# The GLU's first block: four output tiles in shared PSUM banks, multiplied inside the steps of the state-space layer

## The chip, the cores and the metric

The kernel runs on one core of one Trainium2 chip. The metric is the device time of one launch in microseconds (us). Three runs of the kernel before took 2366.6, 2366.81 and 2368.81 us; the median is 2366.81 us. One more execution was profiled and took 2366.55 us; its span between the first and the last instruction is 2364.6 us, and every row below is from it.

## What is computed

The reference is a decoder trunk of two layers on 16 meta tokens and 256 real tokens of width 2048. Layer 0 mixes by attention and a short convolution, layer 1 by a state-space layer (S5) and a gated linear unit (GLU); after each comes a SwiGLU feed-forward network (FFN). The change lies in layer 1, in the state-space layer and the GLU:

```python
# s5_mixer(u, ...), u: (1, 272, 2048)
_, _, x_re, x_im = lax.associative_scan(_complex_affine_combine, (a_r, a_i, bu_re, bu_im), axis=1)
y = einsum('blgp,ghp->blgh', x_re, c_re) - einsum('blgp,ghp->blgh', x_im, c_im)
y = y.reshape(Bsz, L, D_MODEL) + d_skip * uf
g = jax.nn.gelu(y)
return (g @ w_glu1) * jax.nn.sigmoid(g @ w_glu2)      # both weights 2048 x 2048
```

## The kernel before

**Products.** Activations lie transposed in SBUF, as 16 tiles of 128 channels by the tokens. Each is split into a high and a low part (`xh`, `xl`, type fp32r), each weight chunk too (`whi`, `wlo`), and one product of the reference is three matmuls: hi with `xh`, hi with `xl`, lo with `xh` (`mm3`, L297 to L299). The weights come in the order of a plan (class `Weights`): SyncE (SP) loads a chunk into one of four raw buffers, ScalarE (ACT) rounds it to `whi` (L102), VectorE (DVE) subtracts to get `wlo` (L109), both into four buffers. `next` hands a chunk out and first lets `pump` bring casts, subtractions and loads up to `W.ahead` (SA = 3) chunks on. A GLU chunk holds two of the 16 input tiles for all output tiles of its block: three output tiles make it 128x768.

**State-space steps.** The layer works on 16 tiles k of eight groups each. `s5_step(i)` issues for each stage of its list the tile k = i - lag (L1332 on): loads of a tile's tables (`w`, `w2`, `kt`), `f_u` (DVE scales the input), `f_c` (32 small matmuls, L1200), `f_mod` (DVE and GpSimd (POOL) rotate them, L843), `f_scan` (two scans on DVE, L1226, and a rotation), `f_y` (48 small matmuls, L1241 and L1246, into one two-bank tile), `f_yt` (DVE transposes that tile, L1252, which frees it), and the GELU in `f_g1` to `f_g3` over POOL, ACT and DVE. `f_g2` writes `xh` of tile k at step k + 7, `f_g3` writes `xl` at step k + 8. The last stage of tile 15 is in step 23.

**Where steps and GLU meet.** The loop at L1340 issues steps -1 to 17; nothing of the GLU is in them, except that a pump at step 15 brings one cast and one subtraction. Steps 18 to 23 are put into the tick queue `queues[1]` and run, with pauses, between the chunks of the GLU's first block. `GLU_BLOCKS` has four blocks of three output tiles and two of two, each with one PSUM bank per output tile and gate. The order of the chunks in a block is `GLU_ORDER`. When a block's first sums (for the sigmoid) are done, ACT takes their tanh, and DVE multiplies the second sums by it (`gate`); each result is squared for the norm. After the first block everything is drained and PSUM is given out anew.

**Engines.** Each engine works through its own list in order, and the order of issue in the program is that list's order; SP's loads also wait in order, each for its buffer.

Of the kernel before, what the change touches and what calls it, by code (L numbers as in the profile page):

```python
# [10 lines left out]
F32 = mybir.dt.float32  # L11
# [3 lines left out]
AF = mybir.ActivationFunctionType  # L15
ALU = mybir.AluOpType
AX = mybir.AxisListType
PSUM = bass.MemoryType.PSUM
DRAM = bass.MemoryType.DRAM

P = 128
D = 2048
KT = D // P
NMETA = 16
NREAL = 256
# [12 lines left out]
NE = EB + (NC + EB - 1) // EB  # L38
NCP = EB * (NE - EB)
QC = 4 * NC  # L40
GLU_BLOCKS = [(0, 3), (3, 6), (6, 9), (9, 12), (12, 14), (14, 16)]

LOG2E = 1.4426950408889634
LN2_HI = 0.693359375
# [14 lines left out]
WB = 4  # L59
RB = 4  # L60
SA = 3
# [79 lines left out]
def trunk(  # L141
# [5 lines left out]
    nc = tc.nc  # L147
# [8 lines left out]
    W = Weights(nc, raws, parts)  # L156

    def rows(w):
        return w.rearrange("(k p) c -> p k c", p=P)
# [44 lines left out]
    plan_ffn(0)  # L204

    GLU_ORDER = [(c, i) for c in range(6) for i in range(2)] + [(6, 0), (7, 0), (6, 1), (7, 1)]
    for a, b in GLU_BLOCKS:
        for c, i in GLU_ORDER:
            W.add(rows((s5_w_glu2, s5_w_glu1)[i][0])[:, 2 * c:2 * c + 2, a * P:b * P], (2, (b - a) * P))
    plan_ffn(1)  # L210

# [13 lines left out]
    xh = keep.tile([P, KT, NT], F32R, name="xh")  # L225
    xl = keep.tile([P, KT, NT], F32R, name="xl")
# [33 lines left out]
    psm = ps_scope.enter_context(tc.tile_pool(name="psm", bufs=3, space=PSUM))  # L260
# [6 lines left out]
    def bank():  # L267
        return psm.tile([P, 512], F32, tag="mm", name="mm")
# [27 lines left out]
    def mm3(ps, hi, lo, bh, bl, first, last):  # L296
        nc.tensor.matmul(ps, hi, bh, start=first, stop=False)  # L297
        nc.tensor.matmul(ps, hi, bl, start=False, stop=False)  # L298
        nc.tensor.matmul(ps, lo, bh, start=False, stop=last)  # L299
# [77 lines left out]
    queues = [deque() for _ in range(3)]  # L377

    def tick():
        for q in queues:  # L380
            if q:
                for f in q.popleft():
                    f()

    def drain():
        while any(queues):
            tick()

    def warm(func):

        nc.scalar.activation(warm_t, eps_t, func)
# [293 lines left out]
    osq = Squares(KT)  # L685
# [5 lines left out]
    ps2_scope = ExitStack()  # L691
    psm = ps2_scope.enter_context(tc.tile_pool(name="psm2", bufs=8, space=PSUM))
# [116 lines left out]
    CW0 = EW0 + 8 * NCP  # L809
    SCR = CW0 + 8 * 16 * (T + 1)  # L810
# [28 lines left out]
    def ts(o, a, s1, s2, o0, o1, eng=None):  # L839
        (eng or V).tensor_scalar(o, a, s1, s2, op0=o0, op1=o1)  # L840

    def tt(o, a, b, op, eng=None):
        (eng or V).tensor_tensor(o, a, b, op=op)  # L843
# [4 lines left out]
    M_, A_, S_ = ALU.mult, ALU.add, ALU.subtract  # L848
# [304 lines left out]
    osq = ffn(m, Sandwich(m, 0, 1, osq, (0, 2), NT), NT)  # L1153
# [8 lines left out]
    sp_scope = ExitStack()  # L1162
    sp = sp_scope.enter_context(tc.tile_pool(name="sp", bufs=2))
    sps_scope = ExitStack()
    sps = sps_scope.enter_context(tc.tile_pool(name="sps", bufs=1, space=PSUM))
    spx_scope = ExitStack()
    spx = spx_scope.enter_context(tc.tile_pool(name="spx", bufs=3, space=PSUM))

    d0 = [sp.tile([P, 4, NC], F32, name=f"d0{a}", bufs=1) for a in range(2)]
    for a in range(2):  # L1170
# [130 lines left out]
    def read_u(g):  # L1301
        nc.sync.dma_start(out=m_flat[:, 4 * NT * g:4 * NT * (g + 1)], in_=ub[g])

    for k in range(KT + 2):
# [14 lines left out]
        if k == KT + 1:  # L1319
# [3 lines left out]
            for t in range(4):  # L1323
                p = slice(32 * t, 32 * t + 32)
                v = xt[p, :NT].rearrange("p (c s) -> p c s", s=T)
# [6 lines left out]
              (f_g1, 6), (f_scan, 3), (f_yt, 5), (f_y, 4)]  # L1332
    ahead = {f_load: 3, f_load2: 2}

    def s5_step(i):
        for f, lag in stages:
            k = i - lag
            if ahead.get(f, 0) <= k < KT:
                f(k)

    for i in range(-1, KT + 2):
        if i == KT - 1:
            W.pump()
        s5_step(i)
        if i in (2, 4):
            read_u(i // 2 + 1)
    spx_scope.close()


    for i, pause in zip(range(KT + 2, KT + 8), (0, 2, 2, 1, 1, 1)):  # L1350
        queues[1].extend([[]] * pause + [[lambda i=i: s5_step(i)]])
    psg_scope = ExitStack()
    psm = psg_scope.enter_context(tc.tile_pool(name="psg", bufs=6, space=PSUM))
    ps2_scope = ExitStack()
    mr = m[:, :, :NREAL]

    osq = Squares(KT, cols=NREAL)
    ths = {}
    for a, b in GLU_BLOCKS:
        n = b - a  # L1360
        p2 = [bank()[:, :NREAL] for _ in range(n)]
        p1 = [bank()[:, :NREAL] for _ in range(n)]
        now = a == 0 or b == KT
        if b == KT:
            drain()

        def gate(o, a=a, p1=p1):
            tt(mr[:, a + o], p1[o], ths[a][:, o], M_)
            osq.add(mr[:, a + o])
        for c, i in GLU_ORDER:  # L1370
            hi, lo = W.next()
            if c == 7 and i == 1:
                ts(th[:, :n], th[:, :n], 0.5, 0.5, M_, A_)
                if b == KT:
                    warm(AF.Sqrt)
            for o in range(n):
                for k in range(2):
                    kt = 2 * c + k
                    mm3((p2, p1)[i][o], hi[:, k, o * P:(o + 1) * P], lo[:, k, o * P:(o + 1) * P],
                        xh[:, kt, :NREAL], xl[:, kt, :NREAL], kt == 0, kt == KT - 1)  # L1380
                if c == 7 and i == 1 and now:
                    gate(o)
            if c == 7 and i == 0:
                if a == 0:
                    th = sp.tile([P, SCR - CW0], F32, tag="w2", name="th", bufs=3)[:, :3 * NREAL].rearrange("p (o n) -> p o n", o=3)
                else:
                    th = sg.tile([P, 3, NREAL], F32, tag="th", name="th")
                ths[a] = th
                for o in range(n):
                    nc.scalar.activation(th[:, o], p2[o], AF.Tanh, scale=0.5)  # L1390
            tick()
        if not now:
            queues[0].extend([[lambda o=o, g=gate: g(o)] for o in range(n)])
        if a == 0:
            drain()
            psg_scope.close()
            sps_scope.close()
            sp_scope.close()
            sg = ctx.enter_context(tc.tile_pool(name="sg", bufs=2))
            psm = ps2_scope.enter_context(tc.tile_pool(name="psm3", bufs=8, space=PSUM))  # L1400
    act_scope = ExitStack()
    actp = act_scope.enter_context(tc.tile_pool(name="actp2", bufs=1))
    ah = actp.tile([P, 15, NREAL], F32R, name="ah2")
# [113 lines left out]
```

## Time and profile before

| what | value |
|---|---|
| median of three runs | 2366.81 us |
| profiled execution | 2366.55 us (span 2364.6 us) |
| TensorE matmul busy | 2301.9 us, 97% of the span |
| VectorE busy | 1409.7 us, 60% |
| ScalarE busy | 1043.6 us, 44% |
| GpSimd busy | 611.9 us, 26% |
| DMA, mean over the span | 196 GB/s |

A row of a stretch gives the time in us from the span's start, the stretch's length, the busy time of each engine with its number of instructions in brackets, the clock granted to TensorE as a share of its full rate (1.00 is 2.4 GHz, 0.50 is 1.2 GHz), the mean busy share of the DMA engines, and GB/s. A row of the timeline gives start, duration, engine, line and operation, the count of instructions that it merges, and in brackets the idle time before it with what ended it. A row of the chain gives start, duration and the work that the end was traced back to. PE is TensorE.

### The profile page before, as it was taken

How to read it: one execution, taken by the hardware profiler on the slowest of the kernel's cores; microseconds unless marked ns; L12 is line 12 of the kernel's file. 1: busy time of each engine (PE TensorE's matmuls, PEld its weight loads, DVE VectorE, ACT ScalarE, POOL GpSimd, SP SyncE). 2: the span in 40 equal slices, each digit the busy share in tenths (PEclk: the TensorE clock that was granted, in tenths of full speed). 3: DMA queues.
4: the chain of work that ended last, by engine and by line, in shares of the span. 5: the costliest groups of instructions: out<-in, count | busy, mean ns of one | idle time of the engine just before them, and what ended most of it. 6: DMA issues, size and time to landing. Idle time of an engine off the chain costs nothing.

```text
span 2364.6 us, 46794 instructions
## 1 busy us (share of the span) xinstructions
PE 2301.9 (97%) x18838; PEld 2207.0 (93%) x18838; DVE 1409.7 (60%) x2056; ACT 1043.6 (44%) x1582; POOL 611.9 (26%) x811
## 2 busy tenths in 40 slices
PE   8999999999999999999999789999999999999998
PEld 7999999999999999999999569998998999989996
DVE  6555556585755666656755695558555465545565
ACT  5434444553443443333444554446444444434443
POOL 2000001148665667547402350105000000000002
PEclk9999999999999999999999759999999999999999
DMA  6555555456777777777765885555665666655654
GB/s 172 143 152 153 155 151 171 139 155 189 245 235 227 237 228 245 229 229 218 255 212 166 295 312 179 184 176 147 182 201 202 183 184 178 205 184 177 193 192 156
DMA packets 391548, 463.02 MB, mean 196 GB/s; under 512 B 68596, under 2 KB 323092, under 8 KB 391188
## 3 DMA queue, kind: packets, MB, share of 16 engines
q1 hardware_dynamic: 391104, 459.97, 62.9%
q8 instruction: 147, 2.41, 0.4%
q14 instruction: 69, 0.57, 0.1%
q10 hardware_dynamic: 228, 0.08, 0.0%
HBM read 432.37 MB, written 43.32 MB: 201 GB/s over the span
## 4 chain that ended last, share of the span: by engine, by line
PE 90%; DVE 5%; DMA 1%; POOL 1%; ACT 1%; issue 1%; SPq 0%; DVEq 0%; POOLq 0%; ACTq 0%
PE mm L297 23%; PE mm L299 23%; PE mm L298 23%; PE mm L776 5%; PE mm L1443 3%; PE mm L1444 3%; PE mm L1442 3%; DVE wlo L109 1%; PE mm L754 1%; DVE v L1226 1%; PE mm L1062 1%; PE mm L761 1%; PE mm L1079 0%; DMA w<-scr 0%; POOL ct L843 0%
## 5 line engine op out<-in xcount | busy, mean ns | idle before, releaser
L109 DVE TENSOR_TENSOR wlo<-raw,whi 128x768 fp32r<-128x768 f32 (+2 forms) x891 | 945.7, 1074 | 505.2 <-ACT whi L102 497.8
L102 ACT CAST whi<-raw 128x768 fp32r<-128x768 f32 (+2 forms) x891 | 774.1, 884 | 829.1 <-PE mm L298 455.0
L299 PE MATMUL mm<-xh,wlo 128*128 128x272 f32 (+1 forms) x3544 | 1015.7, 287 | 5.5 <-DVE wlo L109 5.5
L297 PE MATMUL mm<-xh,whi 128*128 128x272 f32 (+1 forms) x3544 | 1020.2, 288 | 0.6 <-DVE m L843 0.6
L298 PE MATMUL mm<-xl,whi 128*128 128x272 f32 (+1 forms) x3544 | 1010.0, 285 | 0.0
L299 PEld LDWEIGHTS mm<-xh,wlo 128*128 128x128 f32 x3544 | 670.0, 189 | 7.6 <-DVE wlo L109 7.5
L297 PEld LDWEIGHTS mm<-xh,whi 128*128 128x128 f32 x3544 | 671.3, 189 | 5.3 <-issue 2.8
L298 PEld LDWEIGHTS mm<-xl,whi 128*128 128x128 f32 x3544 | 670.0, 189 | 0.0
L297 PE MATMUL mm<-ah,whi 128*128 128x272 f32 x944 | 274.1, 290 | 0.5 <-ACT m L678 0.5
L299 PE MATMUL mm<-ah,wlo 128*128 128x272 f32 x944 | 273.5, 290 | 0.0
L298 PE MATMUL mm<-al,whi 128*128 128x272 f32 x944 | 271.9, 288 | 0.0
L843 POOL TENSOR_TENSOR m<-m,gb 128x512 f32<-128x512 f32 x8 | 12.1, 1511 | 710.2 <-ACT mm L1456 693.9
L297 PEld LDWEIGHTS mm<-ah,whi 128*128 128x128 f32 x944 | 177.8, 188 | 1.6 <-ACT whi L102 0.8
L299 PEld LDWEIGHTS mm<-ah,wlo 128*128 128x128 f32 x944 | 178.1, 189 | 0.1
L298 PEld LDWEIGHTS mm<-al,whi 128*128 128x128 f32 x944 | 178.2, 189 | 0.0
L314 POOL TENSOR_TENSOR sqacc<-sqacc,sq 128x272 f32<-128x272 f32 (+1 forms) x81 | 85.3, 1053 | 243.3 <-ACT sq L309 241.5
L1443 PE MATMUL mm<-wlo,ah 128*128 128x512 f32 x352 | 137.4, 390 | 1.0 <-DVE wlo L109 1.0
L1442 PE MATMUL mm<-whi,ah 128*128 128x512 f32 x352 | 138.0, 392 | 0.0
L1444 PE MATMUL mm<-whi,al 128*128 128x512 f32 x352 | 137.3, 390 | 0.0
L843 POOL TENSOR_TENSOR bc<-ct,ct 128x64 f32<-128x64 f32 (+2 forms) x128 | 91.3, 733 | 73.1 <-PE mm L1079 69.3
L785 DVE TENSOR_TENSOR gs<-mm,r 128x272 f32<-128x272 f32 (+1 forms) x82 | 35.6, 434 | 107.2 <-PE mm L299 107.2
L582 POOL TENSOR_TENSOR z<-c,x 128x272 f32<-128x272 f32 x8 | 6.3, 783 | 289.8 <-DVE x L575 192.8
(437 smaller groups left out, 2411.4 us busy)
## 6 DMA issues: line engine op xcount, KB each, us to landing
raw<-in_ffn_w_gate_dram SPq DMA_DIRECT2D x224, 384.0 KB, 3.8
raw<-in_ffn_w_up_dram SPq DMA_DIRECT2D x224, 384.0 KB, 4.1
raw<-in_ffn_w_down_dram SPq DMA_DIRECT2D x168, 512.0 KB, 4.8
raw<-in_ab_w_in_dram SPq DMA_DIRECT2D x90, 512.0 KB, 4.1
raw<-in_s_w_glu_dram SPq DMA_DIRECT2D x64, 384.0 KB, 3.7
raw<-in_ab_w_o_dram SPq DMA_DIRECT2D x32, 512.0 KB, 4.5
toep<-taps SPq DMA_DIRECT2D x16, 960.0 KB
w<-scr SPq DMA_DIRECT2D x16, 672.0 KB, 7.6
```

Source lines behind the costliest of these rows:

```text
L102: self.nc.scalar.copy(hi[:, :n], self.raw[i][:, :n])
L109: self.nc.vector.tensor_tensor(lo[:, :n], raw[:, :n], hi[:, :n].bitcast(F32), op=ALU.subtract)
L297: nc.tensor.matmul(ps, hi, bh, start=first, stop=False)
L298: nc.tensor.matmul(ps, hi, bl, start=False, stop=False)
L299: nc.tensor.matmul(ps, lo, bh, start=False, stop=last)
L314: eng.tensor_tensor(self.acc[:, :self.cols], self.acc[:, :self.cols], sq[:, :self.cols], op=ALU.add)
L776: nc.tensor.matmul(pss[o], w[:, k, o * P:(o + 1) * P], xx[:, k, :cols], start=(k == 0 and w is hi and xx is xh), stop=False)
L785: nc.vector.tensor_tensor(gs[:, o, :cols], pss[o], r["r"][:, :cols], op=ALU.mult)
L843: (eng or V).tensor_tensor(o, a, b, op=op)
L1442: nc.tensor.matmul(pss[a], ah[:, kt, ts_], hi[:, k], start=(kt == 0), stop=False)
L1443: nc.tensor.matmul(pss[a], ah[:, kt, ts_], lo[:, k], start=False, stop=False)
L1444: nc.tensor.matmul(pss[a], al[:, kt, ts_], hi[:, k], start=False, stop=(kt == kts - 1))
```

## The change

The first block now has four output tiles (0 to 3), so its chunks are 128x1024; the others have three, three, two, two and two. Its eight sums lie two to a bank: four banks (pool `psb`), which the pool of `f_c` gives up one of its three for. Its 16 chunks go in plain order (c, i), and `first_block` issues one chunk, 24 matmuls, per step from step 9 on, right after `f_g3`, when both input tiles of the chunk are done. The loop runs on to step 23, so the queue of steps 18 to 23 is gone; 15 chunks stand in steps 9 to 23 and one behind them. At step 1 a pump with `W.ahead` = 4 brings two casts, two subtractions and two loads; steps 9 and 10 then need none, and from step 11 on each step brings one cast, one subtraction and one load. Tanh, gate and squares of the four tiles come at the end, two tiles at a time. The second block then starts on banks that the state-space layer has left.

```diff
-GLU_BLOCKS = [(0, 3), (3, 6), (6, 9), (9, 12), (12, 14), (14, 16)]
+GLU_BLOCKS = [(0, 4), (4, 7), (7, 10), (10, 12), (12, 14), (14, 16)]
...
+    GLU_FIRST = [(c, i) for c in range(8) for i in range(2)]
     for a, b in GLU_BLOCKS:
-        for c, i in GLU_ORDER:
+        for c, i in GLU_FIRST if a == 0 else GLU_ORDER:
...
-    spx = spx_scope.enter_context(tc.tile_pool(name="spx", bufs=3, space=PSUM))
+    spx = spx_scope.enter_context(tc.tile_pool(name="spx", bufs=2, space=PSUM))
+    psb_scope = ExitStack()
+    psb = psb_scope.enter_context(tc.tile_pool(name="psb", bufs=4, space=PSUM))
...
-    def s5_step(i):
+    def s5_step(i, also):
         for f, lag in stages:
             k = i - lag
             if ahead.get(f, 0) <= k < KT:
                 f(k)
-
-    for i in range(-1, KT + 2):
-        if i == KT - 1:
+            if f is f_g3:
+                also()
...
+    def first_block(c, i):
+        hi, lo = W.next()
+        for o in range(nb):
+            for k in range(2):
+                kt, ps = 2 * c + k, half(i, o)
+                for w, v in ((hi, xh), (hi, xl), (lo, xh)):
+                    nc.tensor.matmul(ps, w[:, k, o * P:(o + 1) * P], v[:, kt, :NREAL],
+                                     start=(kt == 0 and o % 2 == 0 and w is hi and v is xh), stop=(kt == KT - 1 and w is lo), skip_group_check=True)
...
+        if first and 2 * first[0][0] + 1 <= i - 8:
+            first_block(*first.popleft())
+
+    for i in range(-1, KT + 8):
+        s5_step(i, lambda: some(i))
+        if i == 1:
+            W.ahead = WB
             W.pump()
-        s5_step(i)
+            W.ahead = SA
...
-    for i, pause in zip(range(KT + 2, KT + 8), (0, 2, 2, 1, 1, 1)):
-        queues[1].extend([[]] * pause + [[lambda i=i: s5_step(i)]])
...
+    while first:
+        first_block(*first.popleft())
...
+    for o in range(0, nb, 2):
+        nc.scalar.activation(th[:, o:o + 2], pb[0][o // 2].rearrange("p (o n) -> p o n", o=2), AF.Tanh, scale=0.5)
+    W.pump()
+    ts(th, th, 0.5, 0.5, M_, A_)
+    for o in range(0, nb, 2):
+        tt(mr[:, o:o + 2], pb[1][o // 2].rearrange("p (o n) -> p o n", o=2), th[:, o:o + 2], M_)
```

VectorE, one step in the middle of the layer, before (`rc`, `rs_` from `x` is `f_mod`, `xl` is `f_g3`, `yq` is `f_g2`, `m` is `f_u`, `v` the scans, `yy` the transpose):

```order
L843 TENSOR_TENSOR rc<-x,w 128x272
L843 TENSOR_TENSOR rs__17033<-x,w 128x272
L846 SCALAR_TENSOR_TENSOR xl<-yq,xh 128x8x32
L846 SCALAR_TENSOR_TENSOR yq<-yq,yy 128x256
L843 TENSOR_TENSOR m<-m,r_u 128x8x34
L1226 SCALAR_TENSOR_TENSOR v<-d_16126,z 128x136 x2
L843 TENSOR_TENSOR rc<-v,w 128x272
L843 TENSOR_TENSOR rs__17070<-v,w 128x272
L1252 STREAM_TRANSPOSE yy<-y 128x256
```

and with the change:

```order
L845 TENSOR_TENSOR rc<-x,w 128x272
L845 TENSOR_TENSOR rs__17130<-x,w 128x272
L848 SCALAR_TENSOR_TENSOR xl<-yq,xh 128x8x32
L109 TENSOR_TENSOR wlo_17160<-raw_16059,whi_17048 128x1024
L848 SCALAR_TENSOR_TENSOR yq<-yq,yy 128x256
L845 TENSOR_TENSOR m<-m,r_u 128x8x34
L1230 SCALAR_TENSOR_TENSOR v<-d_16129,z 128x136 x2
L845 TENSOR_TENSOR rc<-v,w 128x272
L845 TENSOR_TENSOR rs__17197<-v,w 128x272
L1256 STREAM_TRANSPOSE yy<-y 128x256
```

One subtraction of 128x1024 has come between `xl` and `yq`, in each step from 11 to 23.

TensorE, two steps in the middle of the layer, before (`x` is `f_c`, `y` is `f_y`):

```order
L1200 MATMUL x<-m,w 64x34 x16
L1241 MATMUL y<-kt,m 32x128 x8
L1246 MATMUL y<-w_16627,xp 32x128 x16
L1200 MATMUL x<-m,w 64x34 x16
L1241 MATMUL y<-kt,m 32x128 x8
```

and with the change, from the end of one step into the next (`g` is a sum of the first block; 24 such matmuls follow one another, then `y` of the step):

```order
L1245 MATMUL y<-kt,m 32x128 x8
L1250 MATMUL y<-w_16805,xp 32x128 x16
L1204 MATMUL x<-m,w 64x34 x16
L1360 MATMUL g<-xh,whi_16342 128x256
L1360 MATMUL g<-xl,whi_16342 128x256
L1360 MATMUL g<-xh,wlo_17050 128x256
L1360 MATMUL g<-xh,whi_16342 128x256
L1360 MATMUL g<-xl,whi_16342 128x256
L1360 MATMUL g<-xh,wlo_17050 128x256
```

The products stand between `f_c` and `f_y`, and `f_y` of the step now waits in order behind them. (The list counts a matmul of fp32 operands once; the profile counts its two passes, 32 for `f_c` and 48 for `f_y`.)

SP's queue at the start of the layer, before:

```order
L1299 DMA ub_4569<-hs 16x8x136 x8
L1176 DMA w<-scr_4496 128x1344
L1302 DMA m<-ub_4568 128x1088
L1176 DMA w<-scr_4497 128x1344
```

and with the change:

```order
L1303 DMA ub_4569<-hs 16x8x136 x8
L96 DMA raw_16346<-in_s_w_glu_dram 128x2x512
L96 DMA raw_16348<-in_s_w_glu_dram 128x2x512
L1180 DMA w<-scr_4496 128x1344
L1306 DMA m<-ub_4568 128x1088
L1180 DMA w<-scr_4497 128x1344
```

Two loads of GLU weights now stand ahead of the fourth tile's table, and each of the two waits for a subtraction of step 1.

## Rows read from the trace of the kernel before

**Rows 1.** Busy time by stretch, from the state-space layer to the end of the GLU

```profile
1340.00:1344.00 4.00, 3.60 (x80) 3.10 (x80) 3.90 (x9) 0.96 (x4) 2.73 (x7) 0.50 1.03 422
1344.00:1347.40 3.40, 2.08 (x76) 1.56 (x68) 3.29 (x9) 0.73 (x2) 1.93 (x4) 1.00 1.01 411
1347.40:1362.00 14.60, 10.81 (x224) 8.34 (x214) 12.05 (x25) 7.22 (x22) 7.96 (x14) 0.50 1.02 411
1362.00:1391.50 29.50, 24.01 (x480) 18.38 (x480) 28.87 (x61) 17.14 (x48) 18.58 (x31) 0.50 0.96 357
1391.50:1406.20 14.70, 10.22 (x208) 7.41 (x208) 14.39 (x29) 9.35 (x25) 9.83 (x16) 0.50 0.90 327
1408.50:1412.20 3.70, 3.70 (x21) 3.70 (x18) 3.01 (x7) 1.89 (x4) 2.28 (x3) 0.50 0.03 13
1412.50:1445.00 32.50, 32.50 (x349) 31.58 (x349) 17.94 (x25) 17.26 (x28) 1.48 (x2) 1.00 0.55 171
1447.50:1596.50 149.00, 148.44 (x1248) 148.27 (x1248) 75.41 (x98) 68.94 (x107) 12.91 (x13) 1.00 0.57 183
```

**Rows 2.** Chain of waits that set the end, in the state-space layer

```profile
1339.61 9.46 DMA w<-scr
...
1386.76 0.33 DVE rc L843
1387.08 0.35 DVE rs__17193 L843
1387.43 0.53 DVE xl L846
1387.96 0.33 DVE yq L846
1388.29 0.63 DVE m L843
1388.92 1.46 DVE v L1226 x2
```

**Rows 3.** Timeline of VectorE: starts of steps 9, 15, 16, 17 and the end of step 18

```profile
1362.01 0.40 DVE L843 TENSOR_TENSOR rc<-x,w 128x272 f32<-128x272 f32 x1
...
1391.55 1.16 DVE L109 TENSOR_TENSOR wlo<-raw,whi 128x768 fp32r<-128x768 f32 x1
1392.63 0.43 DVE L843 TENSOR_TENSOR rc<-x,w 128x272 f32<-128x272 f32 x1
...
1397.19 0.40 DVE L843 TENSOR_TENSOR rc<-x,w 128x272 f32<-128x272 f32 x1
...
1401.73 0.40 DVE L843 TENSOR_TENSOR rc<-x,w 128x272 f32<-128x272 f32 x1
...
1410.03 1.17 DVE L109 TENSOR_TENSOR wlo<-raw,whi 128x768 fp32r<-128x768 f32 x1
```

**Rows 4.** Groups of VectorE's subtraction by shape, whole span (busy us, mean ns)

```profile
L109 DVE TENSOR_TENSOR wlo<-raw,whi 128x768 fp32r<-128x768 f32 x520 | 529.0, 1028 | 316.9 <-ACT whi L102 310.5 <-DMA es<-etabs 2.5 <-PE mm L298 1.9
L109 DVE TENSOR_TENSOR wlo<-raw,whi 128x1024 fp32r<-128x1024 f32 x290 | 360.5, 1260 | 142.8 <-ACT whi L102 142.2 <-PE mm L1443 0.2
```

**Rows 5.** Timeline of TensorE, one step at the low clock

```profile
1372.01 1.08 PE L1241 MATMUL y<-kt,m 128*32 128x128 f32 x16 [0.93 <-DVE yy L1252]
1373.02 1.13 PE L1246 MATMUL y<-w,xp 64*32 64x128 f32 x32
1374.09 1.93 PE L1200 MATMUL x<-m,w 128*64 128x34 f32 x32
```

**Rows 6.** Timeline of TensorE at the clock's rise; first GLU products, 18 up to 1412.26

```profile
1408.47 0.58 PE L297 MATMUL mm<-xh,whi 128*128 128x256 f32 x1
...
1412.26 0.30 PE L299 MATMUL mm<-xh,wlo 128*128 128x256 f32 x1
1412.49 0.65 PE L1241 MATMUL y<-kt,m 128*32 128x128 f32 x16
1413.07 0.69 PE L1246 MATMUL y<-w,xp 64*32 64x128 f32 x32
1413.69 0.39 PE L297 MATMUL mm<-xh,whi 128*128 128x256 f32 x1
```

**Rows 7.** Timeline of TensorE, `f_c` at the high clock and the second block's start

```profile
1344.21 1.13 PE L1200 MATMUL x<-m,w 128*64 128x34 f32 x32
...
1447.99 0.36 PE L297 MATMUL mm<-xh,whi 128*128 128x256 f32 x1 [0.61 <-DVE m L843]
```

**Rows 8.** DMA issues: KB each, median us to landing

```profile
w<-scr SPq DMA_DIRECT2D x16, 672.0 KB, 7.6
...
w<-scr SPq DMA_DIRECT2D x16, 576.0 KB, 5.9
...
kt<-toep SPq DMA_DIRECT2D x16, 512.0 KB, 8.4
```

**Rows 9.** Timeline of VectorE at step 2: idle time ahead of `f_mod`

```profile
1334.69 0.44 DVE L843 TENSOR_TENSOR rc<-x,w 128x272 f32<-128x272 f32 x1 [1.33 <-PE x L1200]
...
1336.39 0.44 DVE L843 TENSOR_TENSOR rc<-x,w 128x272 f32<-128x272 f32 x1 [0.57 <-PE x L1200]
```

**Rows 10.** Busy time by stretch: the clock falls to 0.50 at the end of the second

```profile
1320.00:1323.50 3.50, 2.95 (x10) 1.19 (x8) 3.43 (x9) 3.50 (x9) 1.52 (x2) 0.98 0.94 267
1326.90:1330.30 3.40, 1.76 (x6) 0.59 (x4) 0.49 (x2) 2.53 (x8) 0.00 (x0) 1.00 0.88 206
```

More of the change, by code (lines that the diff above doesn't have):

```diff
@@ L1339, in s5_step, with half, some @@
                 f(k)
-    for i in range(-1, KT + 2):
-        if i == KT - 1:
+            if f is f_g3:
+                also()
+    nb = GLU_BLOCKS[0][1]
+    pb = [[psb.tile([P, 512], F32, tag="g", name="g") for _ in range(nb // 2)] for _ in range(2)]
+    def half(i, o):
+        return pb[i][o // 2][:, NREAL * (o % 2):NREAL * (o % 2 + 1)]
+    def first_block(c, i):
[6 more added lines that the diff above has]
+                                     start=(kt == 0 and o % 2 == 0 and w is hi and v is xh), stop=(kt == KT - 1 and w is lo), skip_group_check=True)
+    first = deque(GLU_FIRST)
+    def some(i):
+        if first and 2 * first[0][0] + 1 <= i - 8:
[4 more added lines that the diff above has]
+            W.ahead = WB
             W.pump()
-        s5_step(i)
+            W.ahead = SA
         if i in (2, 4):
             read_u(i // 2 + 1)
-    spx_scope.close()
-    for i, pause in zip(range(KT + 2, KT + 8), (0, 2, 2, 1, 1, 1)):
-        queues[1].extend([[]] * pause + [[lambda i=i: s5_step(i)]])
-    psg_scope = ExitStack()
-    psm = psg_scope.enter_context(tc.tile_pool(name="psg", bufs=6, space=PSUM))
-    ps2_scope = ExitStack()
+    while first:
+        first_block(*first.popleft())
     mr = m[:, :, :NREAL]
@@ L1358, in trunk @@
     ths = {}
-    for a, b in GLU_BLOCKS:
+    th = sp.tile([P, SCR - CW0], F32, tag="w2", name="th", bufs=3)[:, :nb * NREAL].rearrange("p (o n) -> p o n", o=nb)
+    for o in range(0, nb, 2):
[4 more added lines that the diff above has]
+        tt(mr[:, o:o + 2], pb[1][o // 2].rearrange("p (o n) -> p o n", o=2), th[:, o:o + 2], M_)
+    for o in range(nb):
+        osq.add(mr[:, o])
+    psb_scope.close()
+    spx_scope.close()
+    sps_scope.close()
+    sp_scope.close()
+    sg = ctx.enter_context(tc.tile_pool(name="sg", bufs=2))
+    ps2_scope = ExitStack()
+    psm = ps2_scope.enter_context(tc.tile_pool(name="psm3", bufs=8, space=PSUM))
+    for a, b in GLU_BLOCKS[1:]:
         n = b - a
@@ L1362, in trunk @@
         p1 = [bank()[:, :NREAL] for _ in range(n)]
-        now = a == 0 or b == KT
-        if b == KT:
+        now = b == KT
+        if now:
             drain()
@@ L1373, in trunk @@
                 ts(th[:, :n], th[:, :n], 0.5, 0.5, M_, A_)
-                if b == KT:
+                if now:
                     warm(AF.Sqrt)
@@ L1383, in trunk @@
             if c == 7 and i == 0:
[L1384 to L1388, printed above, removed]
+                th = ths[a] = sg.tile([P, 3, NREAL], F32, tag="th", name="th")
                 for o in range(n):
@@ L1393, in trunk @@
             queues[0].extend([[lambda o=o, g=gate: g(o)] for o in range(n)])
[L1394 to L1400, printed above, removed]
     act_scope = ExitStack()
```

## The prediction

> **What bounds the kernel now.** I read the page first: TensorE is busy nearly everywhere, but its granted clock dips once, past the middle of the span. So I went to the stretches around that dip [rows 1]. From 1340 to 1406 us the clock is 0.50 but for 3.4 us, and from 1362.0 to 1391.5 us VectorE is busy 28.87 of 29.50 us, while TensorE works 24.01 us on little matmuls at half rate. The chain of waits [rows 2] confirms it: first one transfer (`w`, 9.46 us), then one VectorE instruction behind the other. The state-space steps are VectorE's; before 1362 they are the transfers', which run at 411 to 422 GB/s at a share above 1.00 [rows 1]. From 1447.5 us on it is TensorE's: 1248 products in 148.44 us, 0.119 us each, at clock 1.00.
>
> So a GLU product that is moved from behind the steps into them leaves a place where TensorE is the bound for one where it isn't. What counts is what the move costs VectorE, the transfers and the clock.
>
> **The marks.** Before, step 9 begins on VectorE at 1362.01 us and step 15's subtraction at 1391.55: six steps of 4.92 us. That subtraction (768 wide) takes 1.08 us up to the next start, steps 15 and 16 take 4.56 and 4.54, and step 18 ends at 1410.03 [rows 3]. The second GLU block begins at 1447.99 [rows 7], and the products end at 1596.5 [rows 1].
>
> **Start of the layer.** The change puts two loads of 512 KB ahead of the fourth tile's table, where transfers bind. 1.05 MB at 411 to 422 GB/s [rows 1] is 2.5 us. The two early subtractions (2.5 us by their mean, [rows 4]) fall where VectorE is idle for 1.33 and 0.57 us [rows 9], and the steps behind wait for the transfers anyway, so I don't count them again. Bounds: 0 if the loads slip into a gap, 4 if half of the rest of the subtractions and SP's two waits add to it. I take **+2.5 us**, since the share leaves no gap.
>
> **The steps.** Steps 11 to 18 each get a subtraction of 128x1024, eight in all; the one at step 15 goes. The means by shape are 1260 and 1028 ns [rows 4]; scaled by them, 1.08 becomes 1.32 us. Bounds: 1.18 (the mean less the 0.08 us by which the next instruction starts early, 1.16 against 1.08 in rows 3) and 1.5. Sum: 8 x 1.32 - 1.08 = **+9.5 us**. Step 18 then ends at 1410.03 + 2.5 + 9.5 = 1422.0. The casts on ACT are hidden: it is busy 17.14 of 29.50 us [rows 1] and has a step to spare for each. POOL gets nothing.
>
> **What hides the products.** At the high clock TensorE needs per step 1.20 us for `f_y` (1412.49 to 1413.69, [rows 6]), 1.13 for `f_c` [rows 7] and 24 x 0.119 = 2.86 for the chunk: 5.19 us, against VectorE's 4.92 + 1.32 = 6.24. The cover is 1.05 us a step. At the low clock it is 2.08 and 1.93 [rows 5], and 24 x 0.211 = 5.05 (18 products from 1408.47 to 1412.26, [rows 6]): 9.06 us, and the cover is gone. Then `f_y` is late behind its chunk, and after it the transpose on VectorE with all that is queued behind that.
>
> Which clock? With the chunks TensorE at half rate has no idle time left, for 9.06 exceeds 6.24. Unbroken products at half rate brought the clock up within 3.8 us, and it stayed [rows 1, 6]. It held with TensorE busy 2.95 of 3.50 us and fell after a stretch with 1.76 of 3.40 [rows 10]. A step with a chunk at the high clock, 5.19 busy of 6.24, lies nearer to the first. So I expect 1.00 from the first or second chunk on, with a short fall here and there. The Trainium skill, "TensorE: Matmul & The Clock Gate", section "HAM oscillation — how this bites in real kernels", speaks against the change: products in bursts, with waits between them, start each burst at the low clock. By that rule all chunks in the steps would go at half rate, which is the slow rival below. The trace agrees only where TensorE idles about half of the time [rows 10]. I allow **+1.5 us** for what is not made good; bounds 0 and, with the clock low throughout, about 41.
>
> **The tail.** After step 18's transpose TensorE still has two `f_y` and six chunks, and runs them without a break: 2 x 1.20 + 6 x 2.86 = 19.5 us, 21.0 with the 1.5. The last tile's GELU is no later: its `xl` is wanted after four of these chunks, and the operations of `f_yt` to `f_g3` are short beside 8 us. Before, this stretch was 1447.99 - 1410.03 = 38.0. So **-17.0 us**. The second block needs no wait like the 0.61 us for the drain [rows 7], since its first banks were the state-space layer's; tanh and gates run beside its products.
>
> **The rest.** Twelve output tiles in place of thirteen: 1152 for 1248 products, 96 x 0.119 = **-11.4 us**. The smaller block of two tiles costs nothing, by the mean over all blocks in rows 1.
>
> Sum: 2.5 + 9.5 - 17.0 - 11.4 = -16.4 us. Against the profiled execution's 2366.55 that is 2350.2; the median of the runs lies 0.26 higher, so I give **2350.5 us**, 0.7% faster. With all lower bounds (no early delay, 1.18, no clock loss) it is about 2345, with the upper ones (4 us, 1.5 us, 3 us for the clock) about 2355.
>
> **Rivals.**
> - *The clock swings.* Half of TensorE's work in the steps at each rate: (5.19 + 9.06) / 2 = 7.1 us, 0.9 more than VectorE, in nine steps 8 us: 2358.5. For it: the clock rose at 1344 and was back at 0.50 after 3.4 us [rows 1]. Against: then 2.08 of 3.40 us were busy, with little matmuls alone.
> - *The transfers bind further.* Steps 11 to 14 load 1760 KB of tables [rows 8] and now 512 KB of weights. At the 327 GB/s of the last stretch of the steps [rows 1] these 2.33 MB take 7.1 us, 0.9 over VectorE's step, 3.5 us in four steps; with 5 instead of 2.5 us at the start the result is 2356.5. Against: 411 GB/s, where loads were queued, makes 5.7.
> - *The clock stays low, and TensorE becomes the bound of the steps: slower.* Steps 9 to 16 take 9.06 us, steps 17 to 19 without `f_c` 7.13, the last five chunks 5.05: 72.5 + 21.4 + 25.3 from 1364.5 end at 1483.7 in place of 1443.1, 40.6 us later, and the kernel takes 2391. It decides from a TensorE step of about 8.1 us on (16.4 us in nine steps above 6.24), three quarters of the work at half rate. For it: the clock was low in all these steps before. Against: the rise in [rows 6].
> - *The products stand in the steps but gain nothing*, because TensorE, in order, waits there for `xl` and `wlo` and delays `f_y`: within 0.2% of 2366.8. `wlo` comes a step ahead and `xl` early in VectorE's step, so little speaks for it.
>
> **Chances.** Forecast 0.60, swinging clock 0.16, transfers 0.09, low clock 0.07, nothing gained 0.08. A measurement here tells 0.2%, 4.7 us, from no change. Faster 0.84 (the forecast, the swing and the transfers, less 0.01 for a bad mix of these), same 0.09, slower 0.07. The range takes in the first three cases with their bounds: 2345 to 2361 us; outside are the last two and little more.
>
> **What would show it.** Right: clock near 1.00 from about 1375 us on, VectorE's steps of some 6.2 us with one subtraction each, step 9 some 2.5 us later, step 18's end near 1422, the second block's start near 1443 with no idle time before it, and 1152 products at 0.119 us from there. Wrong: clock 0.50 in the steps with TensorE fully busy and VectorE waiting for `f_y`; TensorE waiting for `w` or ACT for raw chunks in steps 11 to 14; or a block start after 1459, which would undo the gain.

## The result and the profile after

The changed kernel takes **2352.34 us** (median of four runs, 2350.43 to 2353.36) beside 2367.81 us for the kernel before (four runs, 2366.6 to 2369.53): a ratio of 0.9933, 95% interval 0.9916 to 0.995. It is faster by 15.5 us where 16.3 were forecast. The profiled execution took 2351.87 us, its span is 2350.1 us.

TensorE's clock, busy time by stretch with the change (the columns of [rows 1]):

```profile
1365.00:1370.00 5.00, 4.16 (x88) 3.22 (x88) 4.89 (x11) 2.88 (x8) 3.12 (x5) 0.50 0.99 385
1370.00:1375.00 5.00, 5.00 (x58) 4.60 (x62) 4.89 (x11) 2.65 (x8) 3.45 (x5) 0.76 0.99 376
1375.00:1380.00 5.00, 5.00 (x104) 4.62 (x102) 4.43 (x9) 2.91 (x8) 3.20 (x5) 1.00 0.70 235
...
1400.00:1405.00 5.00, 4.63 (x100) 3.99 (x99) 4.90 (x10) 2.99 (x8) 3.65 (x5) 1.00 1.03 398
1415.00:1420.00 5.00, 3.56 (x69) 2.96 (x67) 4.90 (x9) 2.99 (x6) 3.30 (x5) 1.00 0.88 315
```

Where rows 1 had 0.50 from 1362 to 1406 us, the clock is now 1.00 from 1375 us on. VectorE (third busy time) stays full: 4.43 to 4.90 of 5.00 us. TensorE is full too until 1400 us, then it has time to spare. So at the end of the steps VectorE is the bound; which of the two binds before 1400 us, these rows alone do not tell (the experiments below do).

VectorE's timeline with the change: the early subtractions, the start of step 9, one whole step, and the first row behind step 18:

```profile
1333.67 2.36 DVE L109 TENSOR_TENSOR wlo<-raw,whi 128x1024 fp32r<-128x1024 f32 x2
...
1366.33 0.40 DVE L845 TENSOR_TENSOR rc<-x,w 128x272 f32<-128x272 f32 x1
...
1389.09 0.41 DVE L845 TENSOR_TENSOR rc<-x,w 128x272 f32<-128x272 f32 x1
...
1390.34 1.51 DVE L109 TENSOR_TENSOR wlo<-raw,whi 128x1024 fp32r<-128x1024 f32 x1
1391.77 0.70 DVE L848 SCALAR_TENSOR_TENSOR yq<-yq,yy 128x256 f32<-128x256 f32 x1
...
1393.29 0.76 DVE L1230 TENSOR_TENSOR_SCAN v<-d,z 128x136 f32<-128x136 f32 x2
...
1395.23 0.40 DVE L845 TENSOR_TENSOR rc<-x,w 128x272 f32<-128x272 f32 x1
...
1423.57 0.84 DVE L848 SCALAR_TENSOR_TENSOR xl<-yq,xh 128x256 fp32r<-128x256 f32 x1
```

Against [rows 3]: step 9 starts 4.3 us later (1366.33 for 1362.01), a step with a subtraction takes 6.14 us (1389.09 to 1395.23), and step 18 ends at 1423.57 for 1410.03. The chain of waits shows the transfers at the start and the tail at the end:

```profile
1338.25 6.52 DMA w<-scr
...
1350.14 9.14 DMA w<-scr
...
1423.70 0.65 PE y L1245 x16
1424.35 0.62 PE y L1250 x32
1424.97 3.04 PE g L1360 x24
1428.01 0.57 PE y L1245 x16
1428.58 0.62 PE y L1250 x32
1429.21 14.46 PE g L1360 x120
...
1443.68 0.70 DVE m L845
...
1444.52 0.36 PE mm L299
```

Six chunks (24 + 120 matmuls) and two `f_y` fill the time from step 18's end to the second block, which starts at 1444.52 in place of 1447.99 [rows 7]. From there to the last gate of the GLU it is 136.8 us (before 148.2). So the gain of some 15 us is made of +4.3 at the start (0.4 of it ahead of the layer), +9.2 in steps 9 to 18, -17.0 in the tail and -11.4 in the rest.

For the experiments, each profile is read at the same marks: **start** is the time from the layer's first product on VectorE (`m`, three rows merged, at 1332.21 before and 1332.61 after) to the `xl` of step 9; **steps** from there to the end of step 18; **tail** from there to the second block's first product. Each ratio is to runs of the kernel before that were made beside that kernel.

| kernel | start | steps | tail | median us | ratio to before, 95% interval |
|---|---|---|---|---|---|
| before | 30.47 | 47.35 | 37.96 | 2367.81 | 1 |
| changed | 34.39 | 56.57 | 20.95 | 2352.34 | 0.9933 [0.9916, 0.995] |
| changed, again | 33.89 | 57.39 | 20.94 | 2351.07 | 0.9935 [0.9922, 0.9947] |
| changed, third | 34.53 | 57.98 | 20.93 | 2350.7 | 0.9932 [0.9918, 0.9946] |
| no early loads | 30.76 | 56.60 | 20.95 | 2348.68 | 0.9925 [0.9912, 0.9939] |
| no early loads, again | 30.91 | 57.74 | 20.95 | 2347.45 | 0.992 [0.9907, 0.9933] |
| no subtraction | 33.39 | 51.12 | 23.22 | 2346.46 | 0.9914 [0.9901, 0.9928] |
| two products of three | 34.95 | 56.05 | 20.95 | 2350.4 | 0.9933 [0.9919, 0.9946] |
| subtraction on GpSimd | 31.12 | 60.20 | 21.76 | 2351.16 | 0.9941 [0.9928, 0.9954] |
| products behind | 34.10 | 46.38 | 49.17 | 2368.97 | 1.0012 [1.0003, 1.0021] |
| three tiles | 33.31 | 54.36 | 17.97 | 2356.02 | 0.996 [0.9947, 0.9973] |
| two in every other step | 33.00 | 62.36 | 25.15 | 2359.5 | 0.9972 [0.9962, 0.9983] |
| other banks | 30.42 | 58.00 | 20.93 | 2347.99 | 0.9919 [0.9906, 0.9933] |

### The profile page after: what moved, and what is told of

Its sections match the earlier page's. It is cut to its first block, busy times and chain, and to the rows that moved or that the text cites. A ratio compares the mean times of both kernels' runs of the same rounds, so it can differ in the third digit from the quotient of the medians.

```text
span 2350.1 us, 46780 instructions
## 1 busy us (share of the span) xinstructions
PE 2287.8 (97%) x18838; PEld 2196.4 (93%) x18838; DVE 1414.6 (60%) x2054; ACT 1044.4 (44%) x1580; POOL 619.7 (26%) x811
## 4 chain that ended last, share of the span: by engine, by line
PE 89%; DVE 6%; ACT 1%; DMA 1%; POOL 1%; issue 1%; SPq 0%; DVEq 0%; POOLq 0%; ACTq 0%
PE mm L299 22%; PE mm L301 22%; PE mm L300 22%; PE mm L778 5%; PE mm L1475 3%; PE mm L1476 3%; PE mm L1474 3%; DVE wlo L109 2%; PE mm L756 1%; PE g L1360 1%; DMA w<-scr 1%; PE mm L1064 1%; PE mm L763 1%; DVE v L1230 0%; PE mm L1081 0%
## 5 line engine op out<-in xcount | busy, mean ns | idle before, releaser
L301 PE MATMUL mm<-xh,wlo 128*128 128x272 f32 (+1 forms) x3416 | 977.0, 286 | 5.9 <-DVE wlo L109 5.9
L299 PE MATMUL mm<-xh,whi 128*128 128x272 f32 (+1 forms) x3416 | 981.3, 287 | 0.9 <-DVE m L845 0.9
L300 PE MATMUL mm<-xl,whi 128*128 128x272 f32 (+1 forms) x3416 | 971.4, 284 | 0.0
L301 PEld LDWEIGHTS mm<-xh,wlo 128*128 128x128 f32 x3416 | 643.5, 188 | 7.6 <-DVE wlo L109 7.6
L299 PEld LDWEIGHTS mm<-xh,whi 128*128 128x128 f32 x3416 | 644.8, 189 | 4.8 <-issue 2.4
L300 PEld LDWEIGHTS mm<-xl,whi 128*128 128x128 f32 x3416 | 643.6, 188 | 0.0
L845 POOL TENSOR_TENSOR bc<-ct,ct 128x64 f32<-128x64 f32 (+2 forms) x128 | 86.4, 696 | 72.7 <-PE mm L1081 68.8
```

## The experiments

**The base.** The changed kernel was run twice more beside its variants.

> The changed kernel itself, unedited, as the base for its variants on the same chip: 2352 us again (2350 to 2354), about 15 us under the kernel before. No theory expects otherwise.

> The changed kernel once more, as the base of the next run on the same chip: 15.5 us under the kernel before, ratio 0.9934.

Measured 2351.07 and 2350.7 us. The three profiles differ most from step 10 to step 11, from `xl` to `xl`: 5.50, 6.69 and 6.95 us, where the kernel before has 4.93. The chain of the third one shows what it is:

```profile
1369.96 5.38 PE g L1360 x24
1375.34 0.57 PE y L1245 x16
```

The first chunk runs at the low clock, 5.38 us for 24 matmuls, and `f_y` stands late behind it. That is the clock's price: 0.6 to 2.0 us, once. The start varies too: over six profiles with the early loads it is 33.00 to 34.95 us, so less than 2 us between two single profiles' starts says little.

**No early loads.** Where does the late step 9 come from, the two loads or the two subtractions?

```diff
-    def pump(self):
+    def pump(self, loads=True):
...
-        self.dma(min(end, self.nl + RB))
+        if loads:
+            self.dma(min(end, self.nl + RB))
...
-            W.pump()
+            W.pump(False)
```

> The early pump after step 1 still makes its casts and subtractions but issues no new raw loads; these come with the first chunk in step 9. Step 9 starts at 1366.33 us of the span in the changed kernel, at 1362.01 in the kernel before. Theory (the two raw loads of 0.5 MB ahead of the fourth table are the delay): step 9 starts back at 1362.0 to 1363.0, and the two loads go into steps 9 to 18, whose transfers moved 390 GB/s on the mean against 413 in the stretch before, so that about 0.35 us is free in each step and the 1.05 MB just fit: 2348 to 2350 us, 2 to 4 under the changed kernel. Rival one (the delay comes from the two early subtractions on VectorE): step 9 stays at 1366 and the time at 2352. Rival two (the steps are at the limit of the transfers): step 9 comes back, and the steps give it back: 2352.

> The version without the early raw loads once more, since 2.4 us could not be told from nothing by the intervals of the first time. By the traces (step 9 starts 3.1 us earlier against the first row of the layer, the steps are as long): 2 to 4 us under the changed kernel of this call, ratio to the kernel before 0.992 to 0.9927. Rival (what was seen is the spread of the runs): the ratio of the changed kernel, 0.9934. Step 9 again starts about 31 us behind the layer's first product on VectorE, against 33.9 to 35.0.

Measured 2348.68 us (2347.72 to 2351.62) and 2347.45 us (2346.09 to 2348.68), 2.4 and 3.3 us under the changed kernel measured beside it (2351.07 and 2350.7). The second time all five runs lie below all five of the changed kernel (2349.3 to 2352.83). The start is 30.76 and 30.91 us where the loads make it 33.89 to 34.53, and the steps are no longer. TensorE's waits for the fourth and the seventh tile's table, first in the changed kernel:

```profile
1344.90 1.93 PE L1204 MATMUL x<-m,w 128*64 128x34 f32 x32 [6.24 <-DMA w<-scr]
...
1359.33 1.93 PE L1204 MATMUL x<-m,w 128*64 128x34 f32 x32 [3.00 <-DMA w<-scr]
```

and without the early loads (the second run):

```profile
1339.21 1.93 PE L1205 MATMUL x<-m,w 128*64 128x34 f32 x32 [2.99 <-DMA w<-scr]
...
1353.72 1.92 PE L1205 MATMUL x<-m,w 128*64 128x34 f32 x32 [1.76 <-DMA w<-scr]
```

The fourth tile's wait, right behind the loads, is the one that shrinks for certain: 6.24, 7.02 and 6.70 us in the three base profiles, 2.85 and 2.99 without the early loads. The later waits overlap (1.71 to 3.00 us for the seventh tile in the base, 3.39 and 1.76 without).

The theory holds: the two loads cost the start 3.4 us (the means are 34.27 and 30.84). The subtractions, made in both, cost little: the four profiles without early loads have 30.42 to 31.12 us, at most 0.7 over the 30.47 before. Loaded in the steps, the same 1.05 MB costs nothing that the times show. This version beats both kernels.

SP's queue shows that the price is more than the bytes. In the changed kernel, and without the early loads (the second run):

```profile
1337.27 0.93 SPq L96 DMA_DIRECT2D raw<-in_s_w_glu_dram  x2
1338.25 0.46 SPq L1180 DMA_DIRECT2D w<-scr  x1
...
1334.98 0.39 SPq L1181 DMA_DIRECT2D w<-scr  x1
```

SP spends 0.93 us on issuing the two loads before it issues the fourth tile's table. That table goes out 5.64 us behind the layer's first product on VectorE (1332.61) in place of 4.49 (behind 1330.49): 1.15 us later, and it then shares the transfers with 1.05 MB more.

**No subtraction.** What binds the steps, and what comes next?

```diff
+        if self.whole[0] <= i < self.whole[1]:
+            self.split[i][1] = hi
+            return
         lo = self.parts.tile([P, CHUNK], F32R, tag="wlo", name=f"wlo{i}")
...
+    W.whole = len(W.plan), len(W.plan) + 16
     for a, b in GLU_BLOCKS:
```

> The 16 chunks of the first block make no low part: the high part stands in its place as third operand, so TensorE's work is the same and VectorE loses a subtraction of 1.43 us in each step. This leaves out the low part of the weights of four output tiles. Theory (VectorE binds the steps, and the transfers come next): a step of 6.15 us cannot fall to 4.72, as its 2.4 MB take 5.8 us at the 413 GB/s of the stretch before; steps of 5.8 us, 8 of them, 2.8 us gained: 2349 us (2347 to 2350), with waits of TensorE or VectorE for transfers in the steps. Rival one (VectorE alone binds): steps of 4.7 us, 8 x 1.43 = 11.4 us gained: 2341. Rival two (TensorE binds, 2.9 us of chunk behind 2.7 to 3.2 us of its own work in a step): steps unchanged: 2352.

Measured 2346.46 us (2345.27 to 2348.0), 4.6 us under the changed kernel (2351.07), between the theory's range and rival one; no theory had that. The steps give 6.2 us, of which the tail takes 2.3 back. The chain changes hands:

```profile
1384.99 0.57 PE y L1249 x16
1385.57 0.62 PE y L1254 x32
1386.19 1.06 PE x L1208 x32
1387.25 3.04 PE g L1364 x24
1390.29 0.57 PE y L1249 x16
```

Every link is TensorE's, 5.30 us a step. So VectorE binds at 6.1 us, and the next limit is TensorE, 0.8 us lower, not the transfers. The expected bound was mis-sized. Its 2.4 MB a step is what 390 GB/s, the mean of steps 9 to 18 in an earlier expectation, moves in 6.15 us. But over these steps the changed kernel moves only 349 GB/s (first row below), and without the subtractions it is 363 GB/s (second row), in 5.3 us 1.9 MB a step:

```profile
1366.00:1424.00 58.00, 54.33 (x988) 47.88 (x992) 56.57 (x105) 35.04 (x85) 37.49 (x50) 0.94 0.93 349
...
1375.00:1412.00 37.00, 37.00 (x728) 33.15 (x728) 33.53 (x67) 25.79 (x63) 22.45 (x35) 1.00 0.96 363
```

The start is 33.39 us with the loads and without the subtractions: once more the loads are the delay.

**Two products of three.** The reverse: less for TensorE, the same for VectorE.

```diff
-                for w, v in ((hi, xh), (hi, xl), (lo, xh)):
+                for w, v in ((hi, xh), (lo, xh)) if c < 5 else ((hi, xh), (hi, xl), (lo, xh)):
```

> The chunks of the steps (the first ten) make two of the three products of a pair, without the low part of the activations against the high part of the weights: 16 matmuls instead of 24, about 1.9 us of TensorE instead of 2.9. Subtractions, transfers and all other work stay. This leaves out that product for k tiles 0 to 9 of four output tiles. Theory (VectorE binds the steps and TensorE's chunks hide): nothing gained, 2351 to 2353, steps of 6.15 us, as long as the clock stays up. Rival one (TensorE binds): 10 x 0.97 = 9.7 us gained, 2342.5. Rival two (the clock is held up only by the full chunks): it falls back to half in some steps, TensorE becomes late, 2355 to 2365.

Measured 2350.4 us (2349.71 to 2353.08), steps 56.05 us: 9.7 us less work for TensorE by the expectation's count, and nothing gained that the noise would not cover. It hides, as the theory says. The clock held through most of the steps with less work than before the edit, then dipped:

```profile
1385.00:1395.00 10.00, 6.86 (x155) 5.64 (x153) 9.79 (x21) 5.77 (x15) 5.37 (x9) 1.00 1.00 378
...
1415.00:1420.00 5.00, 2.80 (x53) 2.22 (x54) 4.89 (x8) 2.57 (x5) 3.21 (x4) 0.77 0.77 286
1420.00:1425.00 5.00, 4.89 (x75) 4.29 (x74) 4.96 (x9) 2.76 (x5) 2.96 (x3) 0.89 0.37 108
```

**Subtraction on GpSimd.** Can VectorE's load be shared? On the version without early loads:

```diff
-        self.nc.vector.tensor_tensor(lo[:, :n], raw[:, :n], hi[:, :n].bitcast(F32), op=ALU.subtract)
+        eng = self.nc.gpsimd if i in self.other else self.nc.vector
+        eng.tensor_tensor(lo[:, :n], raw[:, :n], hi[:, :n].bitcast(F32), op=ALU.subtract)
...
+    W.other = {len(W.plan) + j for j in (5, 7, 9, 11)}
```

> On the version without the early raw loads: four of the ten subtractions that stand in the steps (those of chunks 5, 7, 9 and 11) are made by GpSimd instead of VectorE. VectorE binds the steps by 6.15 us against TensorE's 5.30. GpSimd takes 1.51 us for 128 x 512 in a row of the profile, so about 3.0 us for one of these, and is busy for about 4.1 us of a step now, 1 us of which is stretched beside VectorE's subtraction. Theory (VectorE's sum of work counts): four steps fall from 6.15 to 5.3: 3.4 us under that version, 2345 us. Rival (GpSimd's queue, in order, delays z and yq of the same step by the 3 us, and VectorE waits for them): 0 to 4 x 1.5 us over it, 2349 to 2355.

Measured 2351.16 us (2349.6 to 2353.15); the steps take 60.20 us, 2.5 to 3.6 more than in the version it starts from. The rival's time is right, its reason is not. GpSimd's subtraction is shorter than expected:

```profile
1387.63 2.59 POOL L110 TENSOR_TENSOR wlo<-raw,whi 128x1024 fp32r<-128x1024 f32 x1
```

but VectorE's two scans, beside it, stretch:

```profile
1383.44 0.76 DVE L1233 TENSOR_TENSOR_SCAN v<-d,z 128x136 f32<-128x136 f32 x2
...
1387.89 3.45 DVE L1233 TENSOR_TENSOR_SCAN v<-d,z 128x136 f32<-128x136 f32 x2
1391.45 0.44 DVE L848 TENSOR_TENSOR rc<-v,w 128x272 f32<-128x272 f32 x1
```

Two scans take 0.76 us one step earlier, where VectorE makes the subtraction itself, and 3.45 beside GpSimd's: 2.69 us lost for the 1.43 that the subtraction would have held VectorE. VectorE is not waiting for `z` or `yq`, as the rival has it, but busy in the longer scans. The two engines were in each other's way. The Trainium skill, "Perfetto Trace Analysis", section "Optimizing Scalar/DVE Operations", warns that GpSimd and VectorE share a read port, so that moving work between the two may not help; the trace agrees here, with 3.45 beside 0.76 us.

**Products behind.** Is it the place or the sizes that gains?

```diff
-        if first and 2 * first[0][0] + 1 <= i - 8:
-            first_block(*first.popleft())
+        for _ in range(2 if i >= 18 else 0):
+            if first and 2 * first[0][0] + 1 <= i - 8:
+                first_block(*first.popleft())
```

> No chunk of the first block stands in the steps 9 to 17; from step 18 on two stand in each step and the rest behind the last, as about the same place as in the kernel before; sizes (four tiles, sums in pairs) and the early pump stay. Theory (the place is what gains): the steps lose what the subtractions add, 9.2 us, the tail gets 10 chunks of 2.9 us more and the clock's rise of some 1.5 us again: 21 us over the changed kernel, 2373 us (2369 to 2378). Rival (the gain is from the sizes: 12 instead of 13 tiles behind the layer, fewer gates): 2352.

Measured 2368.97 us (2367.29 to 2369.89), some 18 us over the changed kernel and 3.0 over the kernel before, measured beside it (2365.93). The steps give back 10.9 us beside the mean of the three base profiles (57.3), the tail takes 28.2 more: the theory's mechanism, some 3 us below its figure; 1.7 of that is in the steps, which it put at 9.2. Without chunks the clock is back where it was, and rises only with the products:

```profile
1366.00:1395.00 29.00, 23.37 (x472) 17.75 (x464) 28.37 (x59) 16.76 (x47) 17.77 (x30) 0.50 0.99 373
...
1410.00:1415.00 5.00, 5.00 (x56) 4.62 (x45) 4.66 (x8) 1.93 (x4) 3.37 (x4) 0.65 0.22 85
1415.00:1420.00 5.00, 5.00 (x81) 4.47 (x79) 2.10 (x4) 2.96 (x5) 0.29 (x1) 1.00 0.58 175
```

The sizes alone bring nothing: what twelve tiles save behind the second block's start (11.4 us by the changed kernel), the wider first block costs ahead of it (a tail of 49.17 for 37.96 us).

**Three tiles.**

```diff
-GLU_BLOCKS = [(0, 4), (4, 7), (7, 10), (10, 12), (12, 14), (14, 16)]
+GLU_BLOCKS = [(0, 3), (3, 6), (6, 9), (9, 12), (12, 14), (14, 16)]
...
```

> The first block has three output tiles again, the others those of the kernel before; sums in pairs and products in the steps stay. Theory: the rest behind the layer makes 96 matmul pairs of 0.119 us more, 11.4 us; of that comes back: subtractions of 768 instead of 1024 columns, 0.28 us in each of ten steps, 2.8 us; six chunks of the tail with 18 instead of 24 matmuls, 6 x 0.72 = 4.3 us; smaller early loads, 0.6 us: 3.7 us over the changed kernel, 2355 us (2353 to 2357). Rival (the steps are not bound by the subtraction and the chunk's size costs nothing in them): 11.4 - 4.3 - 0.6 = 6.5 us over, 2358. Rival two (the larger block costs in the steps what it saves behind them): 2352.

Measured 2356.02 us (2354.37 to 2357.11). The time is in the theory's range, but so near to the rivals' that only the marks decide. Steps 2.9 us shorter (2.8 expected), start 0.6 to 1.2 shorter (0.6, but within the spread of the starts), and the GLU from the second block to its last gate 11.6 longer (11.4). The tail gained 3.0 us, not 4.3: with the smaller chunks the clock fell twice, first in the steps and then ahead of the tail:

```profile
1385.00:1390.00 5.00, 3.73 (x81) 2.87 (x81) 4.90 (x10) 3.04 (x8) 3.64 (x5) 0.90 1.00 339
1390.00:1395.00 5.00, 5.00 (x84) 4.40 (x81) 4.89 (x12) 2.97 (x9) 2.55 (x5) 0.76 1.02 388
...
1415.00:1420.00 5.00, 5.00 (x74) 4.38 (x70) 4.96 (x10) 2.85 (x7) 3.04 (x4) 0.66 0.57 201
```

**Two in every other step.**

```diff
-        if first and 2 * first[0][0] + 1 <= i - 8:
+        while first and i % 2 and 2 * first[0][0] + 1 <= i - 8:
             first_block(*first.popleft())
```

> Chunks stand in pairs in the odd steps 9, 11, ... and none in the even ones; all work is the same. In the changed kernel the granted clock is 1.00 from the second chunk to the end of the layer. Theory (TensorE's work of 5.8 us in every other step is enough to keep the clock, and VectorE has the same sum of work): 2351 to 2354, clock 1.00 in the even steps too. Rival (a step without a chunk lets the clock fall to 0.50, and the pair behind it runs at half speed, 11.6 us in two steps of VectorE of 12.3): some us more, 2356 to 2366, with 0.50 to 0.76 in the stretches.

Measured 2359.5 us (2355.71 to 2361.57), about 8.8 us over the changed kernel by the ratios: the rival. The steps grew by 5 us, the tail by 4.

```profile
1395.00:1400.00 5.00, 5.00 (x72) 4.67 (x78) 4.89 (x13) 2.71 (x8) 2.21 (x5) 1.00 1.02 410
1400.00:1405.00 5.00, 3.25 (x112) 2.44 (x92) 4.89 (x11) 2.88 (x10) 3.17 (x6) 0.81 1.03 390
1405.00:1410.00 5.00, 5.00 (x61) 4.64 (x46) 4.71 (x9) 2.78 (x5) 2.97 (x3) 0.50 1.02 409
1410.00:1415.00 5.00, 5.00 (x65) 4.67 (x72) 3.94 (x9) 2.83 (x8) 3.64 (x5) 1.00 0.75 266
```

In the step without a chunk the clock fell, and the next pair began at half rate with VectorE waiting behind it (3.94 of 5.00 us busy). How the loss divides between the clock and the pair's own length, which makes `f_y` wait for two chunks even at the full clock, was not tried apart.

**Other banks.** The prediction saw no wait at the second block's start; there is one of 0.88 us, for the first block's last gate. On the version without early loads:

```diff
+    for _ in range(4):
+        bank()
     for a, b in GLU_BLOCKS[1:]:
```

> On the version without the early raw loads: four PSUM banks are handed out and left unused before the second block, so that its first sums lie in the other four. In the changed kernel the second block's first product waits 0.88 us for the second gate of the first block. Theory (it waits for the bank that this gate reads): the wait goes, the second block starts 0.7 to 0.9 us earlier behind the last product of the first block; too little for the times, which stay within 2346 to 2349 us. Rival (the new pool waits for all of the old one, whichever bank it hands out): the wait stays at 0.88 us.

Measured 2347.99 us (2346.83 to 2348.47), and the wait stays:

```profile
1441.55 0.35 PE L300 MATMUL mm<-xh,whi 128*128 128x256 f32 x1 [0.88 <-DVE m L846]
```

So other banks don't take it away. That the new pool waits for all of the old one, as the rival says, fits this; it was not tried by itself, and the cause stays open.

## Why the prediction was right

**The place.** That the steps are VectorE's and hide TensorE's chunks was the core, and three runs bear it out: a third of the chunks' matmuls taken away gains nothing, the subtraction taken away gains 6 us of the steps, and the chunks put behind the steps cost 18 us.

**Start of the layer.** Forecast +2.5 us, measured +3.4 to +4.1 at the marks in three profiles (33.89 to 34.53 beside 30.47). The mechanism was right: without the loads the delay is 0.3 and 0.4 us in the two runs of that version. The price was mis-sized: 1.05 MB at the full rate is 2.5 us, the loads cost 3.4. The prediction counted bytes alone; SP's queue adds 1.15 us, by which the fourth table is issued later, and that fits the 0.9 us that were missing, though no run tried it by itself.

**The steps.** Forecast +9.5, measured +9.2 (10.0 and 10.6 in the other two profiles of the same kernel), by errors against each other, which is luck. A subtraction in the steps takes 1.51 us and holds the next instruction back by 1.43 (1390.34 to 1391.77), more than the 1.32 taken from the mean over the span. But the step grew only by 1.22 us (6.14 against 4.92), for the two scans became shorter, 0.76 us (at 1393.29) in place of 1.29, while `m` ahead of them became longer, 0.97 in place of 0.71. GpSimd's multiplication of `yq` shows why the scans may be shorter. Before, it runs beside them; with the change it ends at 1393.07, ahead of them:

```profile
1379.00 0.92 POOL L1262 TENSOR_TENSOR yq<-yq,yy 128x256 f32<-128x256 f32 x1
1379.26 1.29 DVE L1226 TENSOR_TENSOR_SCAN v<-d,z 128x136 f32<-128x136 f32 x2
...
1392.15 0.92 POOL L1266 TENSOR_TENSOR yq<-yq,yy 128x256 f32<-128x256 f32 x1
```

The 3.45 us of the scans beside GpSimd's subtraction fit this. The measured steps hold the clock's loss of step 10 as well, which the forecast had put elsewhere.

**The clock.** Forecast 1.00 from about 1375 us, and so it was. The allowance of 1.5 us was put into the tail; it fell in step 10, 0.6 us in the first profile and 1.8 and 2.0 in the others. The rival of the swinging clock, with 0.16, was nearer than the first profile tells: with 18 instead of 24 matmuls a chunk, or with pairs, the clock does fall. But with 16 it held 1.00 until 1415 us, so the number of matmuls alone does not decide, and how near the rival was stays open. The Trainium skill's rule ("TensorE: Matmul & The Clock Gate", section "HAM oscillation — how this bites in real kernels"), cited with the prediction, that bursts with waits between them start at the low clock, does not describe this change: between the chunks TensorE works on the steps' small matmuls, and 1.00 was granted even with 3.56 of 5.00 us busy. The pairs come nearer to it, with 0.50 behind the step without a chunk.

**The tail.** Forecast 21.0 us, measured 20.95, but the parts differ: 20.1 us of work and 0.84 us from the last product to the second block, where the prediction saw no wait. Its reason, "its first banks were the state-space layer's", failed: with other banks the wait stays.

**The rest.** Forecast -11.4 us, measured -11.4.

So the place was right, the tail and the rest came out in their totals, the start was some 1.3 us short, and that the whole came within 1 us is in part luck.

**The rivals.** The transfers that bind further did not come: from 1400 to 1405 us they run at 398 GB/s, TensorE waits for no table in the steps 11 to 18, and 1.05 MB more in them cost nothing. The prediction's cover of TensorE's chunks, 1.05 us a step (5.19 of 6.24), is 0.84 in the runs (5.30 of 6.14), so a lighter VectorE would gain 0.8 us a step and no more.

## What to carry to other kernels

Work that moves under another engine's bound costs what its helpers cost there: here a subtraction of 1.2 to 1.5 us, and loads put ahead of transfers that bound the start. Move each helper to the stretch that has room for it; the same two loads were 3.4 us at the start and nothing in the steps. A filler can keep the clock up, but how much of it is enough was not found: the same chunks in pairs, or a quarter smaller, lost part of the clock again, while chunks with a third fewer matmuls kept it for most of the steps. Test the filler in each form that you mean to use.

## What the runs showed of the hardware that was not expected

VectorE instructions of two fp32 inputs and GpSimd's work beside them lengthened each other here: two scans of 128x136 took 0.76 us with GpSimd idle, 1.29 beside its `yq` and 3.45 beside its subtraction. VectorE's subtraction of 128x1024 took 1.51 us in the steps, where GpSimd is busy 37.49 of 58.00 us, and 1.21 at 1431.52 us in the tail, where it is busy 5.42 of 20.00. GpSimd's `z`, 0.65 us at 1378.39 before, takes 1.46 at 1390.73 beside that subtraction.

TensorE's clock held at 1.00 with 3.56 of 5.00 us busy in the changed kernel and with 6.86 of 10.00 in the one with two products, and went to 0.90 with 3.73 of 5.00 in the one with three tiles. So the busy share of a stretch does not by itself tell the clock.
